# Pairs of SwiGLU blocks by seven products instead of eight, in three phases of a decoder trunk on one Trainium2 core

## The chip, the core and the metric

The kernel runs on one core of a Trainium2 chip. The core has five engines that each execute their own queue in order: PE (TensorE, matrix multiplication), DVE (VectorE), ACT (ScalarE), POOL (GpSimd) and SP (SyncE, here an issuer of transfers only). SP's and POOL's queues start DMA transfers, which then run by themselves. The metric is the device time of one execution in microseconds, lower is better.

## The reference

A decoder trunk of two layers on 256 tokens of width 1024, all in float32. SwiGLU half-steps (f10, f20 in the first layer, f11, f21 in the second) stand before and after a mixer; the first layer's mixer is stick-breaking attention, the second's is sparse attention on shared keys and values.

```python
D_MODEL, SEQ, DEPTH = 1024, 256, 2
D_FF = 2816

def _swiglu(x, w_in, w_out):            # w_in: 1024 x 5632, w_out: 2816 x 1024
    a, b = jnp.split(x @ w_in, 2, axis=-1)
    return (jax.nn.silu(a) * b) @ w_out
...
    for layer in range(DEPTH):
        h = h + 0.5 * _swiglu(_rmsnorm(h, ffn1_norm[layer]), ffn1_w_in[layer], ffn1_w_out[layer])
        hn = _rmsnorm(h, mix_norm[layer])
        if layer < N_A_LAYERS:
            h = h + _stick_breaking_mixer(hn, sb_w_qkv[layer], sb_w_out[layer])
        else:
            h = h + _nsa_mixer(hn, kvs, nsa_w_in[i], nsa_q_norm[i], nsa_w_out[i], cos, sin)
        h = h + 0.5 * _swiglu(_rmsnorm(h, ffn2_norm[layer]), ffn2_w_in[layer], ffn2_w_out[layer])
        if layer == N_A_LAYERS - 1:
            kvs = _nsa_shared_kv(h, ...)
```

## The kernel before

Every fp32 product is made of three matmuls in a reduced format (`mm3`): operand x is split in a high part xh and the rest xl, the weight in wh and wl, and xh·wh + xh·wl + xl·wh are summed in PSUM. The 256 tokens are two tiles (t = 0, 1) of 128.

**Weights** arrive as units of 128x1024 floats (512 KB), in the order in which PE uses them. `Weights` keeps five raw buffers (`wraw`), filled by SP's queue, and six pairs of split buffers: ACT copies raw into `wh` (L119), DVE subtracts it from raw to get `wl` (L125). `pump` puts the split of a unit into the program as soon as a pair of buffers will be free, so a split can run five units ahead of PE. In the dictionary `modes` some out-projection units have another split: in f10 and f20 ten each get `wl` as ACT's negative copy (L121) plus an accumulating DMA of POOL (L122), in f11 ten get `wh` by a casting DMA of POOL (L117).

**A SwiGLU phase** (`ffn`) has 11 blocks. A block is 256 gate columns and 256 up columns: four units, and for each tile 24 matmuls of 512 columns into an `a` bank (48 in all). `gate` then makes `sil` on ACT and `g` on DVE (128x256 each), which frees the bank, and `gtrans` turns the block's `g` by four transposes on PE (`gTp`), with a copy on ACT (L408) and a subtraction on DVE (L409) for its two parts. After the blocks come 22 chunks of the out-projection: a chunk is one unit, 12 matmuls of 512 columns into four `o` banks. Four PSUM banks named `acc` serve the `a` and the `o` in turn; two banks named `z` and two named `aux` serve the rest. `tail` makes the last four chunks for one bank after another, so that the residual, the squares for the next norm and the transposes of h can start. f10 begins with `twin`: blocks 0 and 1 together, in all four `acc` banks, while the weights still arrive; the rms factor (`rss`, `rstd`), which `sil` needs, is made from h (`sqs`, L262; L267 to L272) meanwhile. In f21 the last quarter of each chunk (t = 1, second half) is done as two times 256 columns into two banks.

The order within each engine's queue is set by a scheduler from the written order and priorities; splits have a low priority. It is fixed when the program is built.

Of the kernel before, what the change touches and what calls it, by code (L numbers as in the profile page):

```python
# [61 lines left out]

class Weights:


    def __init__(self, tc, pool, units, raws, bufs):
        self.tc, self.nc, self.pool, self.units = tc, tc.nc, pool, units
        self.raws, self.bufs = raws, bufs
        self.raw, self.hi, self.lo = {}, {}, {}
        self.on_pool = ()  # L70
        self.modes = {}
        self.limit = len(units)
        self.nl = self.ns = self.nt = self.nd = 0

    def load_part(self, j, parts, u=None):
        u = self.nl if u is None else u
        src = self.units[u]
# [4 lines left out]
        self.nc.sync.dma_start(self.raw[u][:, sl], src[:, sl])
        if j == parts - 1:
            self.nl += 1

    def load(self):
        if self.nl < len(self.units):
            self.load_part(0, 1)
# [11 lines left out]

    def pump(self, slack=1, low=LOW):

        u = self.ns
# [8 lines left out]
        raw = self.raw.pop(u)
        prio = self.tc.cur_priority
        self.tc.cur_priority = prio + low
        mode = self.modes.get(u)
        if mode == "cast":
            nc.gpsimd.dma_start(hi[:, 0:n], self.units[u])  # L117
        else:
            nc.scalar.activation(hi[:, 0:n], raw[:, 0:n], AF.Copy)  # L119
        if mode in ("sbuf", "dram"):  # L120
            nc.scalar.activation(lo[:, 0:n], raw[:, 0:n], AF.Copy, scale=-1.0)  # L121
            nc.gpsimd.dma_start(lo[:, 0:n], raw[:, 0:n] if mode == "sbuf" else self.units[u], accum_op=OP.add)  # L122
        else:
            e = nc.gpsimd if u in self.on_pool else nc.vector
            e.tensor_tensor(lo[:, 0:n], raw[:, 0:n], hi[:, 0:n].bitcast(F32), op=OP.subtract)  # L125
# [17 lines left out]
def build(tc, ctx, a, out):
# [234 lines left out]
    def ffn(l, hT, rs, post, targets, side=(), pool=None, start=None):  # L378
        side = list(side)
        with ExitStack() as es:  # L380
            fp = pool or es.enter_context(ffn_pool(l))
            gT, gs = {}, {}

            def part(j):

# [64 lines left out]
            ws = []  # L450
            if start:
                twin()
            else:
                block(0, post, {})
            half = [rs[t][:, 1:2] for t in range(2)]
            for j in range(2 if start else 1, NB):
                at = {1: lambda j=j: gtrans(j - 1)}
# [8 lines left out]

            halves = None if targets else [o[1][1][:, 0:256], aux("o11b")[:, 0:256]]

            def mm(k, t, hf, part_=None):
# [3 lines left out]
                outs = [(o[t][hf], hf * 512, 512)]  # L473
                if halves and t == 1 and hf == 1:
                    outs = [(x, 512 + 256 * i, 256) for i, x in enumerate(halves) if part_ in (None, i)]
                for x, w0, n in outs:
                    mm3(x, gp[0][:, c, t * P:(t + 1) * P], gp[1][:, c, t * P:(t + 1) * P],
                        wh[:, w0:w0 + n], wl[:, w0:w0 + n], k == 0, k == 2 * NB - 1)

            n = 2 * NB - 4  # L480
            for k in range(n):
                ws.append(W.take())
# [862 lines left out]
```

## Time and profile before

| | |
|---|---|
| median of three runs | 1044.95 us (1044.45, 1044.95, 1047.89) |
| profiled execution | 1045.41 us, its span 1043.6 us |
| granted TensorE clock | 0.998 |
| PE instructions counted | 5207 |
| DMA moved | 194.72 MB, mean 187 GB/s |
| loads of 512 KB, issue to landing | 3.5 to 5.0 us (medians by tensor) |

The span is the time from the first to the last instruction of the profiled execution. In rows of the profile, L125 is line 125 of the kernel, `wl<-wraw,wh` names what is written and read, `x298` counts instructions. A group's row gives busy time and the mean of one in ns, then the idle time of its engine right before and which engine's work ended it. In a timeline's row the first number is the start, the second the duration, both in us; the brackets hold the idle time before and its releaser. In a row of windows each engine has its busy time and count, then come the granted clock, the DMA engines' share and GB/s. A row of DMA issues gives count, size and the median time in us from issue to landing.

### The profile page before, as it was taken

What the parts mean: (1) busy time and instruction counts of PE and PEld (TensorE: products, weight loads), DVE (VectorE), ACT (ScalarE), POOL (GpSimd) and SP (SyncE); (2) the same over time, 40 slices, a digit from 0 to 9 for tenths busy, and PEclk for the clock granted to TensorE, in tenths of its full rate; (3) what the DMA queues carried; (4) which work ended last, traced back from release to release, by engine and by line L of the source; (5) the groups of instructions that cost most, each with busy time, mean ns of one, the idle gap of its engine ahead of it and who ended that gap; (6) DMA issues with size and microseconds to landing.
All of it is one profiled execution on the core that took longest, in us unless ns stands there. A gap on an engine that the chain in (4) does not pass through costs nothing.

```text
span 1043.6 us, 14081 instructions
## 1 busy us (share of the span) xinstructions
PE 1030.9 (99%) x5207; PEld 865.3 (83%) x5207; DVE 630.2 (60%) x904; ACT 589.9 (57%) x949; POOL 124.1 (12%) x178
## 2 busy tenths in 40 slices
PE   9999999999999999999999999999989999999998
PEld 6888888899988888888888888778978888888887
DVE  5755423798977555423776586454798665555542
ACT  6645565687866544564565565322689745444431
POOL 0000010120200000010006310100056400000000
PEclk9999999999999999999999999999999999999999
DMA  9855699544335555799555567587540136565651
GB/s 337 272 182 182 190 268 312 164 156 138 106 122 180 183 191 181 212 293 272 170 177 178 182 210 261 175 266 249 163 146 33 41 94 223 175 194 184 188 174 41
DMA packets 55653, 194.72 MB, mean 187 GB/s; under 512 B 6304, under 2 KB 7328, under 8 KB 55584
## 3 DMA queue, kind: packets, MB, share of 16 engines
q1 hardware_dynamic: 50976, 177.93, 51.3%
q0 software_dynamic: 4320, 15.73, 6.9%
q8 instruction: 41, 0.67, 0.3%
q14 instruction: 28, 0.23, 0.1%
q10 hardware_dynamic: 288, 0.16, 0.0%
HBM read 187.50 MB, written 1.05 MB: 181 GB/s over the span
## 4 chain that ended last, share of the span: by engine, by line
PE 92%; DVE 3%; ACT 2%; DMA 1%; issue 1%; SPq 0%; POOL 0%; ACTq 0%; POOLq 0%; DVEq 0%
PE a L169 14%; PE a L171 14%; PE a L170 14%; PE o L169 9%; PE o L170 9%; PE o L171 9%; PE gTp L403 2%; PE S L1002 2%; PE kv L171 1%; PE kv L169 1%; PE kv L170 1%; PE pt L1078 1%; PE hTp L293 1%; PE qk L544 1%; PE a L424 1%
## 5 line engine op out<-in xcount | busy, mean ns | idle before, releaser
L125 DVE TENSOR_TENSOR wl<-wraw,wh 128x1024 fp32r<-128x1024 f32 (+2 forms) x310 | 376.1, 1222 | 286.9 <-ACT wh L119 251.2
L119 ACT ACTIVATE wh<-wraw 128x1024 fp32r<-128x1024 f32 (+1 forms) x322 | 334.2, 1047 | 244.3 <-PE a L171 112.4
L169 PE MATMUL a<-wh,hT_f 128*128 128x512 f32 x528 | 209.4, 397 | 0.0
L171 PE MATMUL a<-wh,hT_f 128*128 128x512 f32 x528 | 206.1, 390 | 0.0
L170 PE MATMUL a<-wl,hT_f 128*128 128x512 f32 x528 | 205.8, 390 | 0.0
L171 PEld LDWEIGHTS a<-wh,hT_f 128*128 128x128 f32 x528 | 99.1, 188 | 21.2
L170 PEld LDWEIGHTS a<-wl,hT_f 128*128 128x128 f32 x528 | 99.3, 188 | 19.5
L169 PEld LDWEIGHTS a<-wh,hT_f 128*128 128x128 f32 x528 | 99.2, 188 | 19.4
L395 ACT ACTIVATE sil<-a,rstd 128x256 f32<-128x256 f32 x86 | 40.6, 473 | 70.6 <-PE a L171 69.2
L169 PE MATMUL o<-wh,gTh0f 128*128 128x512 f32 x192 | 74.0, 385 | 1.9 <-DVE g L396 1.9
L170 PE MATMUL o<-wl,gTh0f 128*128 128x512 f32 x192 | 73.6, 383 | 0.0
L171 PE MATMUL o<-wh,gTl0f 128*128 128x512 f32 x192 | 73.5, 383 | 0.0
L169 PE MATMUL o<-wh,gTh1f 128*128 128x512 f32 (+1 forms) x160 | 61.8, 386 | 0.0
L170 PE MATMUL o<-wl,gTh1f 128*128 128x512 f32 (+1 forms) x160 | 61.3, 383 | 0.0
L171 PE MATMUL o<-wh,gTl1f 128*128 128x512 f32 (+1 forms) x160 | 61.3, 383 | 0.0
L396 DVE TENSOR_TENSOR g<-a,sil 128x256 f32<-128x256 f32 x86 | 36.0, 420 | 41.3 <-ACT sil L395 41.3
L169 PE MATMUL a<-wh,hT 128*128 128x512 f32 x144 | 57.0, 396 | 0.0
L170 PE MATMUL a<-wl,hT 128*128 128x512 f32 x144 | 56.2, 390 | 0.0
L171 PE MATMUL a<-wh,hT 128*128 128x512 f32 x144 | 56.2, 390 | 0.0
L169 PEld LDWEIGHTS o<-wh,gTh0f 128*128 128x128 f32 x192 | 36.1, 188 | 9.5 <-DVE g L396 2.4
L171 PEld LDWEIGHTS o<-wh,gTl0f 128*128 128x128 f32 x192 | 36.0, 188 | 7.1
L170 PEld LDWEIGHTS o<-wl,gTh0f 128*128 128x128 f32 x192 | 36.1, 188 | 7.0
(304 smaller groups left out, 1776.8 us busy)
## 6 DMA issues: line engine op xcount, KB each, us to landing
wraw<-in_f2i SPq DMA_DIRECT2D x88, 512.0 KB, 3.6
wraw<-in_f1i SPq DMA_DIRECT2D x84, 512.0 KB, 4.6
wraw<-in_f1o SPq DMA_DIRECT2D x44, 512.0 KB, 5.0
wraw<-in_f2o SPq DMA_DIRECT2D x44, 512.0 KB, 4.7
wraw<-in_sbqk SPq DMA_DIRECT2D x16, 512.0 KB, 3.5
wraw<-in_kv SPq DMA_DIRECT2D x12, 512.0 KB, 3.9
wl<-wraw POOLq DMA_DIRECT2D x10, 512.0 KB, 6.4
wl<-in_f2o POOLq DMA_DIRECT2D x10, 512.0 KB, 7.6
```

The costliest lines, as they stand in the source:

```text
L119: nc.scalar.activation(hi[:, 0:n], raw[:, 0:n], AF.Copy)
L125: e.tensor_tensor(lo[:, 0:n], raw[:, 0:n], hi[:, 0:n].bitcast(F32), op=OP.subtract)
L169: nc.tensor.matmul(o, xh, wh, start=start, stop=False, skip_group_check=True)
L170: nc.tensor.matmul(o, xh, wl, start=False, stop=False, skip_group_check=True)
L171: nc.tensor.matmul(o, xl, wh, start=False, stop=stop, skip_group_check=True)
L293: nc.tensor.transpose(p[:, c * P:(c + 1) * P], h[:, t, k:k + P], ident)
L395: nc.scalar.activation(sil, o[t][:, 0:256], AF.Silu, scale=rs[t][:, 0:1])
L396: nc.vector.tensor_tensor(g, o[t][:, 256:512], sil, op=OP.mult)
L403: nc.tensor.transpose(p[:, c * 256 + t * P:c * 256 + (t + 1) * P], gs[j, t][:, c * P:(c + 1) * P], ident)
L424: nc.tensor.matmul(o[j][t], x[:, k, t * P:(t + 1) * P], w, start=k == 0 and i == 0, stop=k == 7 and i == 2, skip_group_check=True)
L544: nc.tensor.matmul(oi, wh[:, c], xh, start=k == 0 and q == 0, stop=False, skip_group_check=True)
L1002: nc.tensor.matmul(o, q, k, start=start, stop=False, skip_group_check=True)
```

## The change

In f10, f20 and f21 the last six blocks become three pairs, A, B and C. A pair is a product of x (two tiles t by two halves of K) with four weight blocks of 512 x 512: K half by gate or up. A Strassen form (Winograd's) makes it by seven products for eight. Each product is 12 matmuls of 512 columns with two units of split weight, so a pair has 84 matmuls for 96 and 14 splits for 8. The weights of the seven are, in the order of the products 1, 5, 2, 6, 3, 7, 4: `11`, `12s` (11+12), `21`, `22s` (11+12+22), `22`, `12t` (12+22), `21s` (the sum of all four). The raw blocks stay in four kept tiles of 128x2048, `wk0` to `wk3`, one buffer each, and the sums are made in place: two by DVE (L153, L155) and two by accumulating DMAs of POOL inside SBUF (L156, L181). The sums of x are made once per phase (`xforms`): four DVE operations of 128x512, four copies on ACT, four subtractions on DVE; in f10 `x_parts` first scales xT in place, eight DVE operations of 128x256. The results of the products are put together by ACT copies and DVE additions of 128x512, with `silu` and the gating product on 128x512.

A string per phase (`PLANS`) gives the order of half-blocks (b), transposes (g), products (A1 and so on) and pairs of chunks (c). Chunk c0 now comes before the last blocks; g9 and g10 come after c8. The `modes` are gone; every unit is split by ACT and DVE, but for two that POOL subtracts as before. Loads go up to nine units ahead. f21 does the first 18 chunks with 512 columns and only the last four with two halves.

```diff
+PLANS = {
+    "f10": "b2.0 g0 x b2.1 g1 A1 g2 A5 b3.0 A2 A6 b3.1 A3 b4.0 A7 b4.1 g3 A4 g4 B1 g5 B5 g6 c0 B2 B6 c1 B3 c2 B7 c3 B4 "
+           "c4 C1 g7 C5 g8 c5 C2 C6 c6 C3 C7 c7 C4 c8 g9 g10",
+    "f20": "b0 x b1.0 g0 b1.1 A1 g1 A5 b2.0 A2 A6 b2.1 A3 g2 b3.0 A7 b3.1 A4 b4.0 g3 b4.1 B1 g4 g5 B5 g6 c0 B2 B6 c1 B3 "
+           "c2 B7 c3 B4 c4 C1 g7 C5 g8 c5 C2 C6 c6 C3 C7 c7 C4 c8 g9 g10",
+}
+PLANS["f21"] = PLANS["f20"]
+PRODUCT = {"1": "11", "5": "12s", "2": "21", "6": "22s", "3": "22", "7": "12t", "4": "21s"}
...
+    def form(self, pair, form, q):
+        nc, raw = self.nc, pair.raw
+        if form == "12s" and q == 0:
+            nc.vector.tensor_tensor(raw[0], raw[0], raw[1], op=OP.add)
+        if form == "22s" and q == 0:
+            nc.vector.tensor_tensor(raw[0], raw[0], raw[3], op=OP.add)
+            nc.gpsimd.dma_start(raw[1], raw[3], accum_op=OP.add)
+        return raw[Pair.BASE[form]][:, q * 1024:(q + 1) * 1024]
...
-        mode = self.modes.get(u)
-        if mode == "cast":
-            nc.gpsimd.dma_start(hi[:, 0:n], self.units[u])
-        else:
-            nc.scalar.activation(hi[:, 0:n], raw[:, 0:n], AF.Copy)
-        if mode in ("sbuf", "dram"):
-            nc.scalar.activation(lo[:, 0:n], raw[:, 0:n], AF.Copy, scale=-1.0)
-            nc.gpsimd.dma_start(lo[:, 0:n], raw[:, 0:n] if mode == "sbuf" else self.units[u], accum_op=OP.add)
-        else:
-            e = nc.gpsimd if u in self.on_pool else nc.vector
-            e.tensor_tensor(lo[:, 0:n], raw[:, 0:n], hi[:, 0:n].bitcast(F32), op=OP.subtract)
+        nc.scalar.activation(hi[:, 0:n], raw[:, 0:n], AF.Copy)
+        e = nc.gpsimd if u in self.on_pool else nc.vector
+        e.tensor_tensor(lo[:, 0:n], raw[:, 0:n], hi[:, 0:n].bitcast(F32), op=OP.subtract)
+        if isinstance(x, tuple) and x[1:] == ("22s", 1):
+            nc.gpsimd.dma_start(x[0].raw[0], x[0].raw[2], accum_op=OP.add)
...
+                v.tensor_tensor(d[0], A[1, 1], A[1, 0], op=OP.subtract)
+                v.scalar_tensor_tensor(d[1], d[0], -1.0, A[0, 0], op0=OP.mult, op1=OP.subtract)
+                v.tensor_tensor(d[2], A[0, 0], A[1, 0], op=OP.subtract)
+                v.scalar_tensor_tensor(d[3], d[1], -1.0, A[0, 1], op0=OP.mult, op1=OP.subtract)
+                for i in (0, 1, 3, 2):
+                    nc.scalar.activation(xf[0][:, i], d[i], AF.Copy)
+                    v.tensor_tensor(xf[1][:, i], d[i], xf[0][:, i].bitcast(F32), op=OP.subtract)
...
+            def product(x, m):
+                for q in range(2):
+                    wh, wl = W.take()
+                    for c in range(2):
...
+                        mm3(o, xh, xl, wh[:, c * 512:(c + 1) * 512], wl[:, c * 512:(c + 1) * 512],
+                            k == 0 and m in (1, 2, 5), k == 3 and m in (2, 3, 4))
+                    W.done()
+                    W.pump()
...
+                if m in (1, 5, 6):
+                    nc.scalar.activation(sn({1: 0, 5: 2, 6: 1}[m]), o, AF.Copy)
+                elif m == 2:
+                    nc.vector.tensor_tensor(SN[0], o, SN[0], op=OP.add)
+                    nc.scalar.activation(SN[0], SN[0], AF.Silu, scale=rs[0][:, 0:1])
+                elif m == 3:
+                    nc.vector.tensor_tensor(SN[1], o, SN[1], op=OP.add)
+                    gated(0, SN[1], SN[0])
+                elif m == 7:
+                    nc.vector.tensor_tensor(SN[2], o, SN[2], op=OP.add)
+                else:
+                    nc.scalar.activation(sn(3), o, AF.Silu, scale=rs[1][:, 0:1])
+                    gated(1, SN[2], SN[3])
...
+    def x_parts():
+        for i in range(8):
+            nc.vector.tensor_scalar(xT[:, i, :], xT[:, i, :], vec[:, i:i + 1], None, op0=OP.mult)
```

How the order of instructions moves is shown at three places.

DVE at the start of f10, before: the last splits of the twin blocks, the rms sum, then the next split (the four small rows of each rms factor's rest are left out after the first) and the gate that frees the first `acc` bank.

```order
L125 TENSOR_TENSOR wl_208<-wraw_153,wh_207 128x1024
L125 TENSOR_TENSOR wl_214<-wraw_155,wh_213 128x1024
L125 TENSOR_TENSOR wl_244<-wraw_165,wh_243 128x1024
L267 TENSOR_TENSOR rss<-ssq 128x1
L268 TENSOR_SCALAR rss<-rss 128x1
L271 TENSOR_SCALAR rstd<-rstd 128x1
L125 TENSOR_TENSOR wl_250<-wraw_211,wh_249 128x1024
L396 TENSOR_TENSOR g<-a_179,sil 128x256
```
And in the changed kernel; `xs` are the sums of x, `xff` their low parts, and the gate comes four rows after these:

```order
L179 TENSOR_TENSOR wl_218<-wraw_155,wh_217 128x1024
L541 SCALAR_TENSOR_TENSOR xs_441<-xs_440,xT 128x512
L179 TENSOR_TENSOR wl_260<-wraw_165,wh_259 128x1024
L543 SCALAR_TENSOR_TENSOR xs_443<-xs_441,xT 128x512
L179 TENSOR_TENSOR wl_266<-wraw_167,wh_265 128x1024
L548 TENSOR_TENSOR xff_448<-xs_440,xff_448 128x512
L179 TENSOR_TENSOR wl_294<-wraw_169,wh_293 128x1024
L548 TENSOR_TENSOR xff_448<-xs_441,xff_448 128x512
L548 TENSOR_TENSOR xff_448<-xs_443,xff_448 128x512
L346 TENSOR_TENSOR rss<-ssq 128x1
```
The rms sum (`rss`) now stands behind six operations of x and two more splits.

DVE in the middle of f10, before: a steady stretch of blocks.

```order
L396 TENSOR_TENSOR g_649<-a1_564,sil_648 128x256
L125 TENSOR_TENSOR wl25_673<-wraw25_599,wh25_672 128x1024
L125 TENSOR_TENSOR wl26_685<-wraw26_634,wh26_684 128x1024
L125 TENSOR_TENSOR wl27_720<-wraw27_646,wh27_719 128x1024
L409 TENSOR_TENSOR gTl0f10_396<-gTp_690,gTh0f10_395 128x512
L396 TENSOR_TENSOR g_710<-a0_652,sil_709 128x256
L125 TENSOR_TENSOR wl28_732<-wraw28_676,wh28_731 128x1024
```
The changed kernel where product A4 ends and B begins; `wk0f101` is the first kept tile of pair B, `G` the second gate of pair A, wl35 belongs to B1, wl36 and wl37 to B5:

```order
L179 TENSOR_TENSOR wl35_810<-wk0f101_627,wh35_809 128x1024
L481 TENSOR_TENSOR g_827<-a1_731,sil_826 128x256
L494 TENSOR_TENSOR gTlf10_836<-gTp_830,gThf10_835 128x512
L153 TENSOR_TENSOR wk0f101_627<-wk0f101_627,wk1f101_652 128x2048
L583 SCALAR_TENSOR_TENSOR G_863<-S2_567,S3_861 128x512
L494 TENSOR_TENSOR gTlf10_871<-gTp_865,gThf10_870 128x512
L179 TENSOR_TENSOR wl36_822<-wk0f101_627,wh36_821 128x1024
L494 TENSOR_TENSOR gTlf10_906<-gTp_900,gThf10_905 128x512
L179 TENSOR_TENSOR wl37_846<-wk0f101_627,wh37_845 128x1024
```
Between two splits there now stand a sum over 128x2048, three transposed `g` and a gate.

PE at the end of f20's blocks, before: the last transposes stand after the first chunk, with another chunk behind them that needs only earlier blocks.

```order
L171 MATMUL o11_4176<-wh142_4071,gTl0f20_3320 128x512
L403 MATMUL gTp_4195<-cst_78,g_4141 128x128
L403 MATMUL gTp_4195<-cst_78,g_4170 128x128
L403 MATMUL gTp_4195<-cst_78,g_4141 128x128
L403 MATMUL gTp_4195<-cst_78,g_4170 128x128
L169 MATMUL o00_4173<-wh143_4102,gTh0f20_3319 128x512
L170 MATMUL o00_4173<-wl143_4103,gTh0f20_3319 128x512
L171 MATMUL o00_4173<-wh143_4102,gTl0f20_3320 128x512
```
In the changed kernel the last two blocks' transposes stand right ahead of the chunk that uses them (the rows at L1187 are a mask's, for a later stage):

```order
L488 MATMUL gTp_4625<-cst_78,G_4587 128x128
L488 MATMUL gTp_4634<-cst_78,G_4500 128x128
L488 MATMUL gTp_4634<-cst_78,G_4587 128x128
L488 MATMUL gTp_4634<-cst_78,G_4500 128x128
L488 MATMUL gTp_4634<-cst_78,G_4587 128x128
L1187 LDWEIGHTS identb_114
L1187 MATMUL S1_6991<-mns_118,identb_114 128x288
L237 MATMUL o00_3984<-wh196_4555,gThf20_4630 128x512
L238 MATMUL o00_3984<-wl196_4556,gThf20_4630 128x512
```
The chunk behind the transposes reads `gThf20_4630`, made from the first of the two.

More of the change, by code (lines that the diff above doesn't have):

```diff
@@ L70, in __init__ @@
         self.on_pool = ()
-        self.modes = {}
+        self.kept = None
         self.limit = len(units)
         self.nl = self.ns = self.nt = self.nd = 0
-    def load_part(self, j, parts, u=None):
-        u = self.nl if u is None else u
+        self.loads, self.need, self.order = [], [], {}
+        seen = {}
+        for u, x in enumerate(units):
+            if isinstance(x, tuple):
+                pair, form, q = x
+                if pair not in seen:
+                    seen[pair] = len(self.loads)
+                    self.loads += [(pair, b, y) for b in range(4) for y in range(2)]
+                y = 1 if form in ("12s", "22s") else q
+                self.need.append(seen[pair] + 2 * Pair.NEEDS[form] + y + 1)
+            else:
+                self.order[u] = len(self.order)
+                self.loads.append(u)
+                self.need.append(len(self.loads))
@@ L83, in load_part @@
[L83 to L84 removed]
+        self.nc.sync.dma_start(self.raw_tile(u)[:, sl], src[:, sl])
     def load(self):
[L87 to L88 removed]
+        if self.nl >= len(self.loads):
+            return False
+        x = self.loads[self.nl]
+        if isinstance(x, tuple):
+            pair, b, q = x
+            if self.kept is None:
+                return False
+            if q == 0:
+                pair.raw[b] = self.kept.tile([P, 2048], F32, tag=f"wk{b}", bufs=1, name=f"wk{b}{pair.name}")
+            self.nc.sync.dma_start(pair.raw[b][:, q * 1024:(q + 1) * 1024], pair.src[2 * b + q])
+        else:
+            i = self.order[x]
+            if i >= self.raws and self.rank[i - self.raws] >= self.ns:
+                return False
+            self.load_part(0, 1, x)
@@ L90, in split_part, with ahead @@
+        self.nl += 1
+        return True
+    def ahead(self, n):
+        u = min(self.ns + n, len(self.units) - 1)
+        while self.nl < self.need[u]:
+            if not self.load():
+                return
     def split_part(self, u, j, parts):
@@ L470, in mm @@
+            forms, oo, ws = [], [], {}
+            def mm(k, t, hf, o=None):
+                if k not in ws:
+                    ws[k] = W.take()
                 wh, wl = ws[k]
@@ L472, in mm, with chunk @@
                 c = c0 + k % 2
[L473 to L482, printed above, removed]
+                mm3(oo[t][hf], gp[0][:, c, t * P:(t + 1) * P], gp[1][:, c, t * P:(t + 1) * P],
+                    wh[:, hf * 512:hf * 512 + 512], wl[:, hf * 512:hf * 512 + 512], k == 0, k == 2 * NB - 1)
+            def chunk(k):
                 for t in range(2):
```

209 lines of the change are left out of this document (158 added, 51 removed).

## The prediction

> **What bounds the kernel now.** I read the page's head and busy shares first, then the shares of the chain that ended last.
>
> ```profile
> span 1043.6 us, 14081 instructions
> PE 1030.9 (99%) x5207; PEld 865.3 (83%) x5207; DVE 630.2 (60%) x904; ACT 589.9 (57%) x949; POOL 124.1 (12%) x178
> PE 92%; DVE 3%; ACT 2%; DMA 1%; issue 1%; SPq 0%; POOL 0%; ACTq 0%; POOLq 0%; DVEq 0%
> ```
>
> PE is busy 99% and carries 92% of the chain; DVE and ACT have some 40% to spare on average. So time falls only with PE's work, and it falls by all of it only where DVE, ACT and the DMA still deliver in time. Next, one steady block and the whole of f20 by windows, with the heading of the columns, and PE's timeline inside a stage, for the price of a matmul.
>
> ```profile
> core 0: us, PE busy (x) PEld busy (x) DVE busy (x) ACT busy (x) POOL busy (x), PEclk, DMA share, GB/s
> 335.00:346.35 11.35, 11.35 (x54) 9.40 (x53) 6.31 (x8) 5.58 (x7) 0.00 (x0) 1.00 0.70 226
> 309.00:508.00 199.00, 199.00 (x915) 164.35 (x915) 100.66 (x126) 107.33 (x138) 12.72 (x16) 1.00 0.67 204
> 135.14 0.39 PE L169 MATMUL o<-wh,gTh0f 128*128 128x512 f32 x1
> 135.83 0.39 PE L169 MATMUL o<-wh,gTh0f 128*128 128x512 f32 x1
> 1037.05 0.28 PE L169 MATMUL o<-wh,gTh1f 128*128 128x256 f32 x1
> 1037.40 0.28 PE L169 MATMUL o<-wh,gTh1f 128*128 128x256 f32 x1
> 34.60 0.44 PE gTp L403 x4
> ```
>
> Matmuls overlap: the 0.39 is latency. A block takes 11.35 us; less 0.44 for its four transposes, 10.91 us over 48 matmuls is 0.2273 us each. Three rows apart 135.14 and 135.83 say 0.23. At 256 columns three take 1037.05 to 1037.40, 0.1175 each. The clock column reads 1.00. These are the prices of PE; those of the other engines come from the groups by form:
>
> ```profile
> L125 DVE TENSOR_TENSOR wl<-wraw,wh 128x1024 fp32r<-128x1024 f32 x298 | 365.5, 1235 | 284.6 <-ACT wh L119 249.0 <-DMA wh<-in_f1o 31.0
> L98 DVE TENSOR_TENSOR wl<-wraw,wh 128x512 fp32r<-128x512 f32 x8 | 5.4, 692 | 1.6 <-ACT wh L97 1.5
> L396 DVE TENSOR_TENSOR g<-a,sil 128x256 f32<-128x256 f32 x86 | 36.0, 420 | 41.3 <-ACT sil L395 41.3
> L409 DVE TENSOR_TENSOR gTl0f<-gTp,gTh0f 128x512 fp32r<-128x512 f32 x24 | 16.4, 684 | 0.0
> L119 ACT ACTIVATE wh<-wraw 128x1024 fp32r<-128x1024 f32 x310 | 325.0, 1057 | 239.3 <-PE a L171 112.4 <-PE o L171 52.0 <-PE o11b L171 27.1
> L408 ACT ACTIVATE gTh0f<-gTp 128x512 fp32r<-128x512 f32 x24 | 14.0, 584 | 1.4 <-PE gTp L403 1.3
> 37.93 0.22 DVE L250 TENSOR_SCALAR msb<-msk 128x128 bf16<-128x128 f32 x1
> ```
>
> **What PE gains.** Nine pairs take 84 matmuls for 96: 108 x 0.2273 = 24.5 us. In f21, 108 of 256 columns become 54 of 512: 12.7 - 12.3 = 0.4 us. The third gain is a stall at the start of f11's out-projection:
>
> ```profile
> 679.27 0.39 PE L171 MATMUL o<-wh,gTl0f 128*128 128x512 f32 x1
> 678.84 2.36 DVE L125 TENSOR_TENSOR wl<-wraw,wh 128x1024 fp32r<-128x1024 f32 x2 [4.12 <-DMA wh<-in_f1o]
> 681.12 0.75 DVE L396 TENSOR_TENSOR g<-a,sil 128x256 f32<-128x256 f32 x2
> 681.60 0.50 PE L169 MATMUL o<-wh,gTh0f 128*128 128x512 f32 x1 [1.94 <-DVE g L396]
> 681.93 0.39 PE L170 MATMUL o<-wl,gTh0f 128*128 128x512 f32 x1
> ```
>
> DVE stands 4.12 us before the wl whose wh comes by POOL's cast DMA; the g that frees an o bank is queued behind it, and PE goes from 679.27 to 681.60, 2.33 instead of 0.23. The cast mode goes, ACT makes that wh in 1.06 us: 2.1 us gained. The other twenty special splits (ACT's negative copy, POOL's accumulate) become plain: 1.235 us on DVE per 12 matmuls (2.73 us), hidden by them. Sum of gains: 27.0 us.
>
> **What the pairs put on DVE and ACT.** Per pair DVE has 14 wl (17.3 us) for 8, two sums of 128x2048, three sums and two gates of 128x512. No 2048 form is in the trace: doubling the 1024 row gives 2.47, going on at the slope from 692 to 1235 gives 2.32, the slope alone 2.17; I take 2.32, since the nearest rows show a fixed part. The 512 forms I price at 0.69. A pair by itself is then 17.3 + 4.6 + 3.5 = 25.4 us of DVE against 84 x 0.2273 = 19.1 of PE. What stands between the products must give the 6.3 back. In f20's plan, with their wl, gates and transposed g: from A1 to b4.1 DVE has 26 wl, two sums, five operations of 512, six gates and three transposed g, 32.1 + 4.6 + 3.5 + 2.5 + 2.1 = 44.8, against 228 matmuls and three sets of transposes on PE, 53.1; by the same count from B1 to c4 39.8 against 47.7; and from C1 to C4 34.2 against 36.3. It fits, at 84, 83 and 94%; in before the whole of f20 has DVE at 100.66 of 199 us. Over the program DVE grows by 74 wl (91), 18 sums (42), 69 of 512 columns (48), eight scalings (2), less 36 gates (15): 630 to 798 us. ACT gains 44 copies of 1024 and 57 of 512, less 36 of 256: some 65 us; per pair it stays under PE.
>
> **The accumulate DMAs** (1 MB, two per pair, inside SBUF) and the four kept tiles, one buffer each:
>
> ```profile
> wl<-wraw POOLq DMA_DIRECT2D x10, 512.0 KB, 6.4
> wl<-in_f2o POOLq DMA_DIRECT2D x10, 512.0 KB, 7.6
> wraw<-in_f2i SPq DMA_DIRECT2D x88, 512.0 KB, 3.6
> wraw<-in_f1i SPq DMA_DIRECT2D x8, 256.0 KB, 6.0
> ```
>
> Bounds: 6.4 (size does not matter, as between the 256 and 512 KB loads) to 15.2 (twice the slower); I take 10. The sum for form 12t can be issued once the first sum is done: 96 matmuls (21.8 us) before the split of product 7 in the C stretch, more in A and B. The one for 21s follows the splits of 22s: 78 matmuls (17.7 us) before product 4 in C, 102 (23.2) in A and B. Cost 0. The next pair's load of wk0 waits on SP for the split of 21s, and plain loads stand behind it; six split buffers let the splits run five units ahead (30 product matmuls, 6.8 us), so it is hidden where a half-block or a chunk follows the pair. In f10 A4 is followed by B1 with transposes alone between. There DVE's queue has, from the split ahead to B5's second: a gate, a sum, G, three transposed g, two wl, 0.4 + 2.3 + 0.7 + 2.1 + 2.5 = 8.0, and 0.6 for ACT's part: 8.6 against 6.8, 1.8 us (0 to 4, the load's 3.6 above nothing).
> By the Trainium skill, DMA: Bandwidth & Descriptors, the section on the SWDGE path, such a transfer takes 2.0 us plus its bytes at 436 GB/s, an estimate of 4.4 us for 1 MB; 512 KB would be 3.2 by it, and the trace's 6.4 is twice that, so the trace decides.
>
> **What PE newly waits for.** Most at f10's start. Rows of before:
>
> ```profile
> 14.67 1.69 DVE L1190 SCALAR_TENSOR_TENSOR hT<-xT,vec,hT 128x256 fp32r<-128x256 f32 x4 [0.46 <-ACT hT L1189]
> 16.82 4.83 DVE L125 TENSOR_TENSOR wl<-wraw,wh 128x1024 fp32r<-128x1024 f32 x4 [0.46 <-ACT wh L119]
> 22.12 0.16 DVE L267 TENSOR_TENSOR rss<-ssq 128x1 f32<-128x1 f32 x1 [0.47 <-ACT sqs L262]
> 24.51 1.06 ACT L119 ACTIVATE wh<-wraw 128x1024 fp32r<-128x1024 f32 x1 [0.92 <-DMA wraw<-in_f1i]
> 27.39 0.79 DVE L396 TENSOR_TENSOR g<-a,sil 128x256 f32<-128x256 f32 x2 [0.56 <-ACT sil L395]
> 28.21 0.39 PE L169 MATMUL a<-wh,hT 128*128 128x512 f32 x1
> ```
>
> All four acc banks are taken by the twin blocks; block 2 starts (28.21) when the first g has freed one (27.39). Now the scalings of xT (0.28 each, from the 0.22 row), the x sums and their low parts stand on DVE ahead of rss, and two more wl, whose loads landed for 24.51 and after. From 17.2 (16.36 and three scalings): six wl (7.4), six x operations (4.1), waits for the two late units: rss at about 29 instead of 22.1; then another x low part, rstd, sil, g: a bank free at 31.7. PE waits 3.5 us (1.0, the first wl alone, to 6). In f10's b3.0 two 2048 sums stand on DVE ahead of a wl: 4.6, two wl of 2.5 and 0.9 of gates make 8.0 against the 6.8 in hand: 1.2 (0 to 3). At the starts of f20 and f21 DVE has room:
>
> ```profile
> 327.80 3.50 DVE L125 TENSOR_TENSOR wl<-wraw,wh 128x1024 fp32r<-128x1024 f32 x3 [0.52 <-ACT wh L119]
> 334.81 2.59 DVE L125 TENSOR_TENSOR wl<-wraw,wh 128x1024 fp32r<-128x1024 f32 x2 [2.05 <-ACT wh L119]
> 346.11 2.59 DVE L125 TENSOR_TENSOR wl<-wraw,wh 128x1024 fp32r<-128x1024 f32 x2 [2.49 <-ACT wh L119]
> ```
>
> Eight x operations (5.5 us) meet 0.5 + 2.1 + 2.5 us of idle before these three: 0.4 over, and twice that for what falls too early: 0.8 each, 1.6 (0 to 5). At the phase ends g9 and g10 now stand right ahead of the last chunks, which wait for ACT's 0.58 and DVE's 0.68 behind 0.44 of the second transposes: 0.6, 0.6 and 0.3 = 1.5 (0 to 3). For product sums that stand ahead of a wl on DVE's queue I allow 0.1 per pair, 0.9 (0 to 4).
>
> **Sum.** 3.5 + 1.8 + 1.2 + 1.6 + 1.5 + 0.9 = 10.5 of new waits. 27.0 - 10.5 = 16.5. The profiled execution took 1045.41 us (span 1043.6, 1.8 around it), 0.46 over the median of 1044.95: 1028.9 against it, 1028.4 against the median. I forecast 1028.
>
> **Rivals.**
> (1) DVE becomes the bound. If the covers between products do not reach the products (one queue in order, buffers five units ahead), each pair loses up to 25.4 - 19.1 = 6.3 us, 57 in all: 1028 + 57 = 1085, slower. It decides from 27.0 / 9 = 3.0 us per pair. For it: 94% in the C stretch. Against it: the block's row, with DVE busy 6.3 of 11.35.
> (2) The same in part: only the C stretches and f10 slip, new waits twice mine: 1035 to 1045, centre 1039.
> (3) Hardly any new wait, 0 to 4 us: the idle DVE time of the rows takes it all: 1018 to 1022. Against it: f10's queue at 22.12.
> (4) The accumulates are late. If a pair's two share the engines and take 12 us each, the second lands 24 us after its issue, 6.3 late in C and 0.8 in A and B: 3 x 6.3 + 6 x 0.8 = 24 us, 1052, slower; it decides at 11.6 us each, where C alone loses 3 x 5.5 = 16.5. For it: the 7.6 for half the bytes; against it: the loads, whose time hardly follows size, and that the first can go early.
> (5) PE runs slower after f10's stall:
>
> ```profile
> 0.98 4.45 PE L232 MATMUL warm<-wz 128*128 128x512 bf16 x10 [0.98 <-POOL mhalf L237]
> 0.98:5.43 4.45, 4.45 (x11) 1.71 (x12) 0.87 (x2) 2.76 (x4) 0.13 (x1) 1.00 0.79 224
> ```
>
> Here, after idle time, ten matmuls took 0.445 each, though the granted clock reads 1.00. If a stall of 3.5 us brings that back for as long, it costs 10 x (0.445 - 0.227) = 2.2 us: 1031. The 2.33 us gap at 679 did not: the two behind it stand 0.33 apart (681.60, 681.93).
> That is the clock gate of the Trainium skill, TensorE: Matmul & The Clock Gate, Part 1: half clock after an idle window of about 3.4 us, windows running freely. The trace agrees on the half rate at the start; whether 3.5 us of waiting holds a whole window no row here shows.
>
> **How the numbers follow.** Forecast 0.62, its own range 1022 to 1035, from waits of 4 to 17 us within the bounds above; (5) 0.06; (3) 0.10; (2) 0.12; (1) 0.06; (4) 0.04. A change under 0.3% (3.1 us) can't be told from none here: that is 1041.8 to 1048.1. Faster: 0.62 + 0.06 + 0.10 + two thirds of (2), 0.86; same 0.05, the rest of (2) and a little of (1); slower 0.09. Range 1019 to 1041, leaving out a sliver of (3) and (1), (4), the top of (2).
>
> **What would show it.** Right: some 5060 PE matmuls, DVE near 800 us, wl of 1.235 and sums near 2.3; a PE gap of 3 to 4 us at 28, no gap at f11's out-projection; accumulates landing in about 10 us with no split of 12t or 21s named as waiting for them. Wrong: PE waiting for wl in every pair with DVE never idle (1); splits waiting for an accumulate or a wk load (4); another matmul spacing inside products than 0.227.

## The result, and the profile after

The changed kernel takes 1029.08 us (median of three, 1028.9 to 1029.43) against 1044.95: 0.984 of the time before (95% interval 0.981 to 0.987). 1028 was forecast. Its page's head and busy shares:

```profile
span 1027.7 us, 13963 instructions
PE 1007.5 (98%) x5045; PEld 842.2 (82%) x5045; DVE 780.5 (76%) x1038; ACT 648.4 (63%) x1014; POOL 119.3 (12%) x166
PE 80%; DVE 8%; issue 6%; ACT 2%; DMA 2%; POOL 0%; SPq 0%; ACTq 0%; DVEq 0%; POOLq 0%
```

PE lost 23 us of busy time, the span only 15.9. DVE gained 150 us and took 8% of the chain in place of 3%: some of the work that was to be hidden now ends waits. The groups by form and the DMA issues show what the new operations cost:

```profile
L179 DVE TENSOR_TENSOR wl<-wraw,wh 128x1024 fp32r<-128x1024 f32 x246 | 301.3, 1233 | 101.4 <-ACT wh L177 98.7
L153 DVE TENSOR_TENSOR wk0f<-wk0f,wk1f 128x2048 f32<-128x2048 f32 x9 | 20.6, 2290 | 0.2
L583 DVE SCALAR_TENSOR_TENSOR G<-S,S 128x512 f32<-128x512 f32 x18 | 12.3, 684 | 0.0
```

```profile
wk1f<-wk3f POOLq DMA_DIRECT2D x9, 1024.0 KB, 7.5
wk0f<-wk2f POOLq DMA_DIRECT2D x9, 1024.0 KB, 8.9
```

The sums take 2.29 us (2.32 was taken), the operations of 512 columns 0.68, the accumulates 7.5 and 8.9 (10 was taken). No split is named as waiting for an accumulate. Splits do wait for loads of the kept tiles, which the prediction had named as a sign of being wrong (from the list of waits: total, times, longest, in us):

```profile
ACT wh L177 <- DMA wk0f<-in_f1p: 8.0, 4, 5.0
ACT wh L177 <- DMA wk0f<-in_f2p: 5.2, 3, 2.5
```

The stages, from the starts of their first matmuls in PE's timeline (us; the sum of the differences is that of the spans; the forecast is the prediction's terms, put to the stage that each belongs to):

| stage | before | after | difference | forecast |
|---|---|---|---|---|
| f10 (to the first `v`) | 192.91 | 192.58 | -0.3 | -0.8 |
| stick | 124.99 | 127.29 | +2.3 | 0 |
| f20 | 186.76 | 179.54 | -7.2 | -6.5 |
| key/value phase and f11 | 237.34 | 235.14 | -2.2 | -2.1 |
| nsa | 111.28 | 111.66 | +0.4 | 0 |
| f21 | 186.53 | 177.70 | -8.8 | -7.2 |

Three pairs are worth 36 matmuls, 8.2 us. f20 keeps most of it and f21 all. In f20 PE is busy 178.90 of 179.54 us with DVE at 80%, as one row of windows (same columns as ahead) shows, and its only wait is at the phase end, in PE's timeline:

```profile
319.87:499.41 179.54, 178.90 (x821) 147.96 (x819) 143.78 (x154) 111.41 (x137) 6.86 (x9) 1.00 0.71 229
487.07 0.50 PE L237 MATMUL o<-wh,gThf 128*128 128x512 f32 x1 [0.64 <-ACT gThf L493]
```

f10 keeps almost nothing. PE's rows with a wait, in order of time (the bracket holds the idle time behind the modelled end of the matmul before; what the text calls a wait or gap is, where starts show it, the time from start to start beyond the usual 0.23; the matmul after the first one behind a wait starts another 0.1 late, which is not counted):

```profile
30.68 0.50 PE L237 MATMUL a<-wh,hT 128*128 128x512 f32 x1 [1.70 <-DVE g L481]
...
49.75 0.50 PE L238 MATMUL a<-wl,hT 128*128 128x512 f32 x1 [0.54 <-DVE wl L179]
...
87.19 0.55 PE L488 MATMUL gTp<-cst,g 128*128 128x128 f32 x3 [1.05 <-DVE g L481]
...
92.39 0.50 PE L238 MATMUL pc<-wl,xff 128*128 128x512 f32 x1 [0.32 <-DVE wl L179]
94.31 0.50 PE L238 MATMUL pc<-wl,xff 128*128 128x512 f32 x1 [0.27 <-DVE wl L179]
```

Block 2 starts 2.5 us later than the 28.21 of before; b3.0 loses 1.1 (49.75 and a second wait at 51.65), the place where pair A meets pair B 2.3. These two places were forecast at 1.2 and 1.8. What the rows don't say is what made DVE late.

### The profile page after: what moved, and what is told of

Read it like the earlier page. It is cut to its first block, busy times and chain, and to the rows that moved or that the text cites. A ratio compares the mean times of both kernels' runs of the same rounds, so it can differ in the third digit from the quotient of the medians.

```text
span 1027.7 us, 13963 instructions
## 1 busy us (share of the span) xinstructions
PE 1007.5 (98%) x5045; PEld 842.2 (82%) x5045; DVE 780.5 (76%) x1038; ACT 648.4 (63%) x1014; POOL 119.3 (12%) x166
## 3 DMA queue, kind: packets, MB, share of 16 engines
q1 hardware_dynamic: 50976, 177.93, 49.2%
## 4 chain that ended last, share of the span: by engine, by line
PE 80%; DVE 8%; issue 6%; ACT 2%; DMA 2%; POOL 0%; SPq 0%; ACTq 0%; DVEq 0%; POOLq 0%
PE a L238 8%; PE a L237 8%; PE a L239 8%; PE o L237 8%; PE o L239 8%; PE o L238 8%; DVE wl L179 3%; PE pa L238 2%; PE pa L239 2%; PE pa L237 2%; PE S L1187 2%; ACT wh L177 1%; PE gTp L488 1%; PE pc L238 1%; PE pc L239 1%
## 5 line engine op out<-in xcount | busy, mean ns | idle before, releaser
L179 DVE TENSOR_TENSOR wl<-wraw,wh 128x1024 fp32r<-128x1024 f32 (+1 forms) x258 | 311.9, 1218 | 105.4 <-ACT wh L177 102.7
L177 ACT ACTIVATE wh<-wraw 128x1024 fp32r<-128x1024 f32 (+2 forms) x260 | 268.7, 1044 | 139.1 <-PE o L239 71.0
L237 PE MATMUL a<-wh,hT_f 128*128 128x512 f32 x336 | 133.4, 397 | 0.0
L239 PE MATMUL a<-wh,hT_f 128*128 128x512 f32 x336 | 131.1, 390 | 0.0
L238 PE MATMUL a<-wl,hT_f 128*128 128x512 f32 x336 | 131.0, 390 | 0.0
L177 ACT ACTIVATE wh<-wk0f 128x1024 fp32r<-128x1024 f32 x72 | 75.4, 1058 | 66.1 <-DVE wk0f L153 20.7
L179 DVE TENSOR_TENSOR wl<-wk0f,wh 128x1024 fp32r<-128x1024 f32 x72 | 87.0, 1221 | 34.8 <-ACT wh L177 33.8
L237 PE MATMUL o<-wh,gThf 128*128 128x512 f32 (+1 forms) x264 | 102.7, 391 | 1.4 <-ACT gThf L493 1.4
L238 PE MATMUL o<-wl,gThf 128*128 128x512 f32 (+1 forms) x264 | 102.6, 389 | 0.0
L239 PE MATMUL o<-wh,gTlf 128*128 128x512 f32 (+1 forms) x264 | 102.1, 389 | 0.0
L729 PE MATMUL qk<-hT_m,wh 128*128 128x256 f32 x128 | 37.1, 290 | 0.0
L730 PE MATMUL qk<-hT_m,wh 128*128 128x256 f32 x128 | 36.2, 283 | 0.0
```

Source lines behind the costliest of these rows:

```text
L237: nc.tensor.matmul(o, xh, wh, start=start, stop=False, skip_group_check=True)
L238: nc.tensor.matmul(o, xh, wl, start=False, stop=False, skip_group_check=True)
L239: nc.tensor.matmul(o, xl, wh, start=False, stop=stop, skip_group_check=True)
L729: nc.tensor.matmul(oi, wh[:, c], xh, start=k == 0 and q == 0, stop=False, skip_group_check=True)
L730: nc.tensor.matmul(oi, wh[:, c], xl, start=False, stop=False, skip_group_check=True)
```

## The experiments

Times of the runs below go by their own comparisons with the kernel before; stage times are read as in the table.

**1. The plain splits alone.** The kernel before, without its special splits:

```diff
-    W.modes = modes
+    W.modes = {}
```

> The kernel before, with every out-projection unit split by ACT and DVE (no accumulating or casting DMA of POOL for weights). Theory: only the stall at the start of f11's out-projection goes (681.60), 2.1 us; the twenty units of f10 and f20 cost DVE 25 us that PE covers. 1042.9 us, last PE start at 1037.7, no row at L396 that PE waits for. Rival: the POOL splits were a relief that DVE needs; then PE waits for wl in the chunks and the time is 1045 or more.

Measured: 1043.2 us, 0.996 of before (0.995 to 0.998). f11's stage is 235.14 in place of 237.34, f20's is the same (186.76), and no wait for L396 is left on PE. So the 2.2 us of f11 belong to the casting DMA, as forecast, and the twenty accumulating splits were not worth anything.

**2. f10 with plain blocks,** pairs in f20 and f21 alone:

```diff
-    "f10": "b2.0 g0 x b2.1 g1 A1 ...",
...
```

(The rest of the edit gives f10 its plain list of units and its plain loop over blocks.)

> The changed kernel with f10 in plain blocks (its order of steps as in the kernel before), pairs in f20 and f21 alone. Theory: f10's three pairs were worth 36 matmuls (8.2 us) and lost as much in waits, so leaving them out costs 0 to 1 us: first v matmul near 193.5, total 1029 to 1030; if the 2.3 us that stick takes longer come from the way f10's end was reordered, 1027 to 1028. Rival (gains add up, waits lie elsewhere): 1037.

Measured: 1027.5 us (0.982, 0.980 to 0.983), `v` at 194.94 (193.5 was expected), stick 124.94. As expected, in the second form: f10's three pairs brought 2.4 us to f10 and lost them in stick. But this kernel makes no x sums in f10, and block 2 still starts at 30.37. ACT's timeline of this run:

```profile
24.66 1.06 ACT L177 ACTIVATE wh<-wraw 128x1024 fp32r<-128x1024 f32 x1 [2.58 <-DMA wraw<-in_f1i]
25.95 0.63 ACT L344 ACTIVATE sqs<-h 128x512 bf16<-128x512 f32 x1 [0.22 <-DMA h<-in_x]
```

Here the squares wait for the load of h, not for DVE: its halves land at 25.86 and 28.69, against 20.52 and 21.86 before. In the changed kernel they land at 23.92 and 25.24, and the squares wait for something else. ACT's and DVE's rows there:

```profile
24.14 0.63 ACT L547 ACTIVATE xff<-xs 128x512 fp32r<-128x512 f32 x1 [2.28 <-DVE xs L543]
24.67 1.05 ACT L177 ACTIVATE wh<-wraw 128x1024 fp32r<-128x1024 f32 x1
25.63 0.61 ACT L547 ACTIVATE xff<-xs 128x512 fp32r<-128x512 f32 x1
26.14 0.61 ACT L341 ACTIVATE sqs<-h 128x512 bf16<-128x512 f32 x1
...
26.90 1.29 DVE L548 TENSOR_TENSOR xff<-xs,xff 128x512 fp32r<-128x512 f32 x2
28.10 0.15 DVE L346 TENSOR_TENSOR rss<-ssq 128x1 f32<-128x1 f32 x1
```

ACT stands for an x sum of DVE and makes the squares 2.2 us after h has landed, and DVE has no idle time from 17.41 to rss at 28.10.

**3. h ahead of the look-ahead loads.** In SP's timeline of the changed kernel, and of the one before, h stands here:

```profile
6.98 12.00 SPq L111 DMA_DIRECT2D wraw<-in_f1i  x6
19.04 0.90 SPq L1390 DMA_DIRECT2D h<-in_x  x2
```

```profile
7.70 6.22 SPq L82 DMA_DIRECT2D wraw<-in_f1i  x4
13.98 0.90 SPq L1205 DMA_DIRECT2D h<-in_x  x2
```

`AHEAD` put two more weight loads in front, and they wait for raw buffers.

```diff
+    for t in range(2):
+        nc.sync.dma_start(h[:, t, :], a["x"][t])
     W.pump(low=0)
     split_x(6, 2)
-    for t in range(2):
-        nc.sync.dma_start(h[:, t, :], a["x"][t])
```

> The changed kernel with the two loads of h issued on SP ahead of the loads that the greater look-ahead added (h was issued at 19.04 instead of 13.98). Theory A (f10's late second start comes from the x operations queued on DVE ahead of the rms sum): block 2 still starts about 30 us or, as far as the order on DVE changes with it, somewhat earlier, 1028 to 1029. Theory B (h lands late behind two weight loads on SP, and the squares and the gate with it): block 2 starts near 28.9, 1027.2.

Measured: block 2 at 28.65, all but 0.4 of the start's loss gone, `v` 1.4 us earlier; the wait at b3.0 grew to 1.8. The time is 1029.2 (1027.3 to 1029.8), no change beyond the interval (0.981 to 0.984), since nsa took 1.0 longer in the profile. The edit touches nothing in nsa, but in every trace the granted clock falls to a half there for a while, here for longer than in the changed kernel (one row of windows of each; PE alone: busy time, clock, DMA share, GB/s):

```profile
767.45:774.28 6.83, 6.25 (x24) 0.50 0.24 80
769.90:773.31 3.41, 3.31 (x11) 0.50 0.02 5
```

Of the fourteen traces of this case six have 3.4 us of it, and nsa takes 111.3 to 112.0; eight have 6.8, and nsa takes 112.1 to 113.0. With h early the scheduler also put the rms sum ahead of most x operations, so this run alone does not separate the two causes. Run 2 shows that a late h is enough without x operations.

**4. The x operations after the gates:**

```diff
...
-            nc.vector.tensor_scalar(xT[:, i, :], xT[:, i, :], vec[:, i:i + 1], None, op0=OP.mult)
+        v = rp.tile([P, 16], F32, tag="rss", bufs=4, name="vx")[:, 0:8]
+        nc.vector.scalar_tensor_tensor(v, g[:, 0:8], 0.0, vec[:, 0:8], op0=OP.mult, op1=OP.add)
+            nc.vector.tensor_scalar(xT[:, i, :], xT[:, i, :], v[:, i:i + 1], None, op0=OP.mult)
```

(`g` is the last gate of the twin blocks, which the function now gets.)

> The changed kernel with the scalings of xT made to wait for the last gate of the twin blocks (their factors are copied through an operation that reads it), so no x operation stands ahead of the rms sum or the gates; the loads of h stay where they are. Theory A (DVE's queue): block 2 starts at 28.8 to 29.2, 1.5 to 2.1 us are gained at the start, up to 1 us comes back where the x operations now stand ahead of the first pair's splits: 1027 to 1028. Theory B (h late on SP): block 2 still starts at 30 or later, 1029 or more.

Measured: 1032.7 us (0.987, 0.985 to 0.988), worse than both theories. Block 2 starts at 28.60, as theory A had it. The first half of h lands at 24.08, as late as in the changed kernel (23.92), so the 2.1 us between 30.68 and 28.60 belong to the x operations; the squares start at 24.16, right behind it. But the x operations now stand ahead of pair A's splits, PE waits 1.35 us at 45.4 and 2.25 at 49.3, and meanwhile something else happens. PE's timeline and the windows around it (PE alone, columns as in run 3):

```profile
28.60 0.50 PE L237 MATMUL a<-wh,hT 128*128 128x512 f32 x1 [0.32 <-DVE g L481]
...
45.40 0.50 PE L238 MATMUL pa<-wl,hT 128*128 128x512 f32 x1 [1.18 <-DVE wl L179]
...
46.37 0.63 PE L238 MATMUL pa<-wl,hT 128*128 128x512 f32 x1
46.80 0.63 PE L239 MATMUL pa<-wh,hT 128*128 128x512 f32 x1
49.28 0.80 PE L237 MATMUL pc<-wh,xff 128*128 128x512 f32 x1 [1.85 <-ACT wh L177]
...
51.56 0.63 PE L237 MATMUL pc<-wh,xff 128*128 128x512 f32 x1
51.99 0.63 PE L238 MATMUL pc<-wl,xff 128*128 128x512 f32 x1
```

```profile
42.57:45.98 3.41, 2.05 (x10) 1.00 0.60 238
45.98:49.39 3.41, 1.56 (x5) 0.50 0.02 10
49.39:52.81 3.42, 2.96 (x6) 0.50 0.95 192
52.81:56.22 3.41, 3.41 (x9) 0.50 0.92 214
56.00:58.00 2.00, 2.00 (x10) 0.95 0.99 395
```

From 46 to 56 the granted clock is 0.50 and matmuls are 0.43 us apart: a second loss of some 3.4 us (17 matmuls, 0.2 more each).

**5. All four sums on DVE:**

```diff
-            nc.gpsimd.dma_start(raw[1], raw[3], accum_op=OP.add)
+            nc.vector.tensor_tensor(raw[1], raw[1], raw[3], op=OP.add)
...
-            nc.gpsimd.dma_start(x[0].raw[0], x[0].raw[2], accum_op=OP.add)
+            nc.vector.tensor_tensor(x[0].raw[0], x[0].raw[0], x[0].raw[2], op=OP.add)
```

> The changed kernel with all four weight sums of a pair on DVE (18 more operations of 128x2048, 2.29 us each; no accumulating DMA). A test of how near DVE is to being the bound: by the count of the prediction DVE then has 49.4 us against PE's 53.1 in the A stretch, 44.4 against 47.7 in B, 38.8 against 36.3 in C. Theory: the C stretches lose 2.5 us each and f10, which already waits, 1 to 3 more: 1029 + 9 to 12 = 1038 to 1041. Rival (DVE is in truth the bound wherever products run): 4.6 us for each of nine pairs, 1070. Rival (there is slack everywhere): 1029 to 1031.

Measured: 1030.1 us (0.985, 0.983 to 0.986), 1 us over the changed kernel; f20 179.82, f21 177.93, 0.3 and 0.2 more. 41 us more on DVE cost nothing that counts. f20's row:

```profile
319.00:499.00 180.00, 179.36 (x819) 148.01 (x818) 156.74 (x160) 111.44 (x137) 1.48 (x2) 1.00 0.55 193
```

At 156.7 of 180 us DVE is still covered. My theory fell: a count over one stretch of the plan (38.8 against 36.3) is too strict, presumably because the splits can run ahead into stretches with chunks.

**6 and 7. A new end of f10, and c0 between A4 and B1** (both with h first; run 7 has the new end too):

```diff
-... c0 B2 B6 c1 B3 c2 B7 c3 B4 c4 C1 g7 C5 g8 c5 C2 C6 c6 C3 C7 c7 C4 c8 g9 g10
+... c0 B2 B6 c1 B3 c2 B7 c3 B4 c4 C1 g7 C5 g8 c5 C2 C6 c6 C3 C7 C4 c7 g9 g10 c8
```

> The changed kernel with the loads of h ahead of the look-ahead loads (as the run before with that edit) and f10's plan ended by C7 C4 c7 g9 g10 c8 in place of C7 c7 C4 c8 g9 g10, so that a chunk follows the last transposes. In the build, stick's instructions then stand on DVE in the order of the kernel before. Theory: the 0.7 us wait at f10's end goes and stick takes 124.9 us again in place of 127.3: 2.4 + 0.7 less than with the h edit alone, 1024.5 in the profile's span. Rival (stick's 2.3 us come from how full the buffers are when it starts, not from the order): 1026.7.

Measured: 1025.4 us (0.980, 0.978 to 0.981); stick 125.04, f10's end without a wait. Run 3, with h first and the old end, still had 127.3, so stick's 2.3 us come from the order of its instructions on DVE, which f10's end had changed. In the changed kernel DVE, POOL and PE have these rows there:

```profile
221.08 1.23 DVE L179 TENSOR_TENSOR wl<-wraw,wh 128x1024 fp32r<-128x1024 f32 x1 [0.28 <-ACT wh L177]
222.22 1.62 DVE L783 TENSOR_TENSOR spx<-s,spx 128x384 fp32r<-128x384 f32 x1
...
222.06 1.37 POOL L751 TENSOR_TENSOR qkT<-qk,qkT 64x512 fp32r<-64x512 f32 x1 [6.97 <-ACT qkT L748]
...
223.90 0.45 PE L791 MATMUL z<-spx,negU 128*128 128x384 f32 x1 [1.41 <-DVE spx L783]
```

A split went ahead of `spx`, which then ran beside POOL's `qkT` and took 1.62 us for its usual 0.55; PE waited for it. In run 6:

```profile
217.45 0.55 DVE L783 TENSOR_TENSOR spx<-s,spx 128x384 fp32r<-128x384 f32 x1
217.92 1.23 DVE L179 TENSOR_TENSOR wl<-wraw,wh 128x1024 fp32r<-128x1024 f32 x1
219.07 1.51 DVE L754 TENSOR_TENSOR qkT<-qk,qkT 64x256 fp32r<-64x256 f32 x1
```

Here another operation meets POOL, one that nobody waits for. By the Trainium skill, SBUF — State Buffer, the section on the two sides of SBUF, of a DVE operation with two SBUF inputs and a POOL operation that reads SBUF, the one that starts first holds up the other until it ends. The stretched rows agree with it: POOL's ends at 223.43, `spx` at 223.84.

```diff
-... g3 A4 g4 B1 g5 B5 g6 c0 B2 B6 ...
+... g3 A4 c0 g4 B1 g5 B5 g6 B2 B6 ...
```

> As the run with h first and the new end of f10, and besides c0 stands between A4 and B1 in f10 (24 matmuls, 5.5 us, in place of after g6). Theory: the waits where pair A meets pair B (2.3 us in the trace of the changed kernel, at 87 to 94) go, since DVE's sum, transposed g and splits of 8.6 us then meet 12 us of PE work: 2 us less, span 1022.5. Rival (the wait only moves to B2, whose splits lose the cover that c0 gave): no change, 1024.5.

Measured: 1023.8 us (0.979, 0.977 to 0.980), f10 1.7 us shorter; 0.4 and 0.9 came back at B2 and near f10's end. What made the place late in the changed kernel is in ACT's timeline:

```profile
83.23 1.06 ACT L177 ACTIVATE wh<-wk0f 128x1024 fp32r<-128x1024 f32 x1 [2.62 <-DMA wk0f<-in_f1p]
84.48 1.06 ACT L177 ACTIVATE wh<-wk0f 128x1024 fp32r<-128x1024 f32 x1 [0.19 <-DMA wk0f<-in_f1p]
```

The single buffer wk0 could be loaded only at 77.04, after pair A's last split, and its halves landed 6 and 7 us later; g, sum and splits of B stood behind that.

**8. All four sums by POOL:**

```diff
-            nc.vector.tensor_tensor(raw[0], raw[0], raw[1], op=OP.add)
+            nc.gpsimd.dma_start(raw[0], raw[1], accum_op=OP.add)
...
-            nc.vector.tensor_tensor(raw[0], raw[0], raw[3], op=OP.add)
+            nc.gpsimd.dma_start(raw[0], raw[3], accum_op=OP.add)
```

> The changed kernel with all four weight sums of a pair as accumulating DMAs of POOL (36 of 1 MB; DVE freed of 18 sums, 41 us). The first two sums are needed two and four units after the split that releases them, with six split buffers, so 7 to 9 us of transfer cannot hide there. Theory (an accumulate is free only by its distance): each of the first two comes 2 to 4 us late in most pairs, 1029 + 9 x 5 = 1075 (1050 to 1100). Rival (DVE's sums are what delays; transfers hide anyway): 1025.

Measured: 1100.1 us (1.051, 1.049 to 1.053), the theory's upper end. The list of waits:

```profile
ACT wh L177 <- DMA wk0f<-wk3f: 59.7, 9, 8.1
ACT wh L177 <- DMA wk0f<-wk1f: 51.2, 8, 8.1
```

The accumulates with some 18 us or more of PE's work (the prediction's count) between issue and use cost nothing; those that are needed two to four units later cost ACT more than 6 us each. Nothing between was tried. The profile's mean granted clock is 0.974, against 0.998 in the changed kernel, so a part of the loss is half rate behind such waits.

**9 to 12. Other plans of f10** (all with h first and a changed end, stick at 124.9 to 125.0; 9, 10 and 12 with c0 ahead of B1). 9: `A1 b3.0 g2 A5 A2 b3.1 A6 A3 b4.0 A7`. 10: `b3.0 A1 g2 A5 b3.1 A2 A6 b4.0 A3 b4.1 A7 g3 c0 A4 g4 c1 B1`, B with one chunk pair less. 11: two pairs only, after b4. 12: `b3.0 A1 ... b4.0 A3 A7 b4.1 g3 A4 c0 g4 B1 ... C2 C6 C3 C7 c6 C4 c7 g9 g10 c8`.

> As the run with c0 between A4 and B1 (1023.8), with f10's A stretch in the order A1 b3.0 g2 A5 A2 b3.1 A6 A3 b4.0 A7, so that a half-block follows A1 and the split of b3.0 stands on DVE ahead of the second sum. Theory (the 1.8 us wait at 49 comes from the two sums of 2.29 us that stand ahead of that split): it goes, 1022.0. Rival (the two sums delay A5 or A6 instead, the wait moves): 1023.8.

Measured: 1024.6 us (0.979, 0.977 to 0.981). The wait stayed: PE waits 1.68 us at 46.17, for ACT's `wh` of b3.0, with the second sum now behind it. So not the sums alone made that place late. ACT's timeline of this run:

```profile
44.09 0.60 ACT L587 ACTIVATE S<-pa 128x512 f32<-128x512 f32 x1 [2.17 <-PE pa L238]
44.58 0.59 ACT L492 ACTIVATE gThf<-gTp 128x512 fp32r<-128x512 f32 x1
45.06 2.00 ACT L177 ACTIVATE wh<-wraw 128x1024 fp32r<-128x1024 f32 x2
```

The two loads of b3.0 had landed at 39.8 and 41.1. ACT's copies of them stand in its queue behind the copy of A1's result, which waits for PE.

> As the run before this one, but with b3.0 ahead of A1, the half-blocks one place earlier, and c0 and c1 at the end of the A stretch, so that B has one chunk pair less (B7 and B4 stand together). Theory: the wait at 49 goes, but in B the splits of 21s follow those of 12t with 12 matmuls between and DVE has 39.8 us against some 42: 1022 to 1023. Rival (B loses its cover): 1025 or more.

Measured: 1027.6 us (0.982, 0.980 to 0.984): the wait at 49 is gone (0.15 left), with b3.0 ahead of A1. But C's wk0 arrives late (ACT waits 4.95 us for `wk0f<-in_f1p` at 125.95), PE stands 4.6 us before 128.92, and matmuls run at half the clock until 134.

> The changed kernel with h first and two pairs in f10 in place of three (blocks 7 to 10), the products starting only after b4. 12 more matmuls (2.7 us) than with three pairs. Theory: f10 then has no waits but those of its start (0.6), so that it takes 192.9 - 5.5 + 0.3 = 187.7 to v against 188.6 with three pairs and c0 moved: 1022.9. Rival (waits of a pair are the same wherever it stands): 1026.

Measured: 1023.1 us (0.978, 0.976 to 0.980), `v` at 187.76 (187.7 was expected): with the products later, f10 has no waits but the start's.

> f10 planned anew from what the runs before showed, three pairs: h's loads first; b3.0 ahead of A1, so that its weights are loaded ahead of the four kept tiles; A3 A7 b4.1 g3 A4 c0 at the end of A, so that b4.1 stands between the last two products on the same bank and c0 between A4 and B1; C2 C6 C3 C7 c6 C4 c7 g9 g10 c8 at the end, so that c6 stands between C7 and C4. Theory: of the waits of the run with c0 between A4 and B1 (v at 188.6) the one at 49 (1.8) and the one at 163 (0.9) go: v at 186.0, span 1019.1, time 1021. Rival (the loads of pairs A and B collide as in the run with two chunks in A, or A7 waits for its accumulate with A3 alone ahead of it): 1024 or more.

Measured: 1023.4 us (0.978, 0.977 to 0.980), `v` at 188.19. The waits at 49 and 163 went, but one of 2.2 us came at 97.8: B2 needs the bank of a transposed `g`, whose subtraction stands behind the second sum on DVE. The best time of all is that of runs 7, 11 and 12, which their intervals do not separate: 0.978 to 0.979 of before, 5 to 6 us under the changed kernel.

## Why the prediction was right or wrong

- **Matmuls.** 108 fewer at 0.2273 us: f20 and f21 show it (-7.2, -8.8); in f10 the waits took it back. Right.
- **f11's stall.** 2.1 forecast, 2.2 measured, and run 1 shows the cast as its cause.
- **f10's start.** 3.5 forecast, 2.5 measured. The mechanism is in the trace: the six splits and six x operations that were counted stand ahead of rss, which comes at 28.10 (about 29 was forecast), and a bank is free at 30.63 (31.7). The waits for two late units, which the count had added, did not come. Run 4 gives the x operations 2.1 us. What the step did not see is a second cause beside the first: `AHEAD` moved two loads past h on SP's queue, and run 2 shows that this alone delays the start by as much. With both there, they do not add up.
- **b3.0 and A4 to B1.** 1.2 and 1.8 forecast, 1.1 and 2.3 measured. At b3.0 the count of DVE's queue was part of it (the second sum ends at 47.96, right ahead of a transposed `g` and the first wl at 48.48). The second wl waits for ACT's `wh`, which stands behind the copy of a product's result, as in run 9; the loads had landed at 41.3 and 42.6. Between A4 and B1 the load of wk0 follows the last split of the pair, and DVE's queue starts behind it: "the load's 3.6 above nothing" should have been its landing of 6.
- **f20's and f21's starts.** 1.6 forecast, no gap found. **Phase ends:** 1.5 forecast, 0.7, 0.8 and 0.4 measured. **The sums ahead of wl,** 0.9: no such wait in f20 and f21.
- **stick and nsa.** Nothing forecast, 2.3 and 0.4 lost. For stick the step that failed is the silence on stages whose code is the same: the order of their queues was not looked at. nsa's 0.4 lies within the 111.3 to 112.0 that it takes in the traces with 3.4 us of half rate; no run shows a cause for it.
- Sum: 10.5 of losses forecast, 11.1 measured (27.0 - 15.9). The sum was nearer than its terms: stick, nsa and the phase ends made up for the start and for terms that did not come, which is luck.
- **Rivals.** (1) DVE as the bound fell by run 5; (2) and (3) by the sum of 11.1; (4) by the 7.5 and 8.9 us; (5) did not come at 28, where PE stood 1.9 us, but did in runs 4 and 10.

## What to carry to other kernels

Work that PE no longer does is gained where other engines have slack in that very stage, and f10, at the start of the program, had little: there two pairs that begin later did as well as three. When an edit adds loads or look-ahead, follow every queue that it lengthens (here SP's, ahead of h) and every single buffer whose next load waits for a last reader. Two causes can each be enough for the same wait, and taking one away then shows only a part of the other: look at what the late operation waited for in the kernel itself, not in a variant of it. And compare the order of instructions in the stages that were not edited: a scheduler may move them, at a price of the same size as a term of the sum.

## What the runs showed of the hardware

The clock fell after less waiting than I had assumed it would need: in run 4 it read 0.50 from about 46, behind a single gap of 1.35 us (PE busy 2.05 of the 3.41 us ahead), and came back after some 10 us; in run 10 a gap of 4.6 us was followed by some 5 us at half rate. But in the kernel before, the 3.41 us from 677.92 to 681.33 have PE busy for only 1.73 and no fall behind them, so how idle PE must be cannot be read off these figures. The 2.1 us gap of the kernel before (681.60) and the 1.9 at 30.68 brought nothing of the kind. By the Trainium skill, TensorE: Matmul & The Clock Gate, Part 1, an idle window of 3.4 us, at a moving phase, is what halves the clock; run 10's gap is longer than that, though the clock fell some 2.8 us into it, at 127.25; run 4 has no idle of that length, so there the measurement decides. The falls inside the kernels last 3.4, 6.8 or 10.2 us, one to three times the same length; what decides between one and two in nsa is open, and it goes with some 1 us of the time. And two kinds of DVE operation stretch to three times their time beside a POOL operation (`spx` 0.55 to 1.62 us, `qkT` 0.42 to 1.51), which hurts only the one that PE waits for.
